# Compressed branch's readout with all 128 rows of the array: a block-sparse attention layer on one core

## The chip, the cores and the metric

The kernel runs on one core of one Trainium2 chip, as one launch. The time is device microseconds of an execution; the value of a kernel is the median of its runs. Of the engines, TensorE does the matmuls (each a weight load, "PEld" in the profile, and a pass of the moving operand, "PE"), VectorE (DVE), ScalarE (ACT) and GpSimd (POOL) do the rest, and SyncE (SP) issues most DMAs.

## What is computed

A trunk of two layers over 256 tokens of width 1024: a gated delta-rule layer (8 heads of 128), then an attention layer with 16 heads of 64 in 4 groups that share keys and values. The second layer has three branches, and its output is a gated sum of them. The change touches the compressed branch alone:

```python
p_cmp = masked_softmax(sc, cmp_end[None, :] <= t[:, None])
o_cmp = jnp.einsum('bgrqn,bgnd->bgrqd', p_cmp, v_cmp)
...
o = jnp.stack([o_cmp, o_sel, o_win], axis=2).astype(jnp.float32)
o = jnp.sum(gates[..., None] * o * jax.nn.silu(z.astype(jnp.float32)), axis=2).astype(x.dtype)
return o.reshape(b_sz, t_len, NSA_WIDTH) @ w_out
```

The keys and values of this branch are blocks of 32 tokens at a stride of 16, so there are 15 of them for 256 tokens; the kernel keeps 16 per head, the last one masked. With 4 blocks of 64 tokens and 16 to be chosen, the selection branch attends to all visible tokens.

## The kernel before

All activations are in float32. A projection is made of three matmuls on a high and a low part: L233 (high weights, high input), L234 (high weights, low input) and L235 (low weights, high input). Weights come as tiles of 128x1024 by DMA, ScalarE makes the high part (`hi_...`, L181) and GpSimd the low part (`lo_...`, L185). All engines but SyncE run in the order in which the program is written, so a list of small tasks is interleaved by hand: `fill(n)` takes the next n pieces of a projection from a list and puts them at this place of TensorE's order, and `defer(n, f)` puts a task n steps later.

In the attention of the second layer the work goes by units. A unit is a pair of heads for the first 128 tokens, or one head for the second 128. For each unit, in the order given by a string of digits: `scores` (L1327, TensorE), `maxima` (VectorE adds the mask and takes maxima, L1336 to L1343), `exps` (ScalarE, L1356 to L1361; `pt` holds the two long branches, `Pc` the compressed one), `transposes` (L1369 for the long branches, L1371 for `Pc`), `probs` (ScalarE copies the transposed probabilities out of PSUM, L1376 and L1380), and then, for each pair of heads, `readout`. Between them `fill` puts the pieces of the gate projection (`bz`) and of the output projection (`bo`).

`readout` multiplies the transposed probabilities by the values. The long branches take 4 or 8 matmuls with all 128 keys of a block as rows (L1395 for the first half of the tokens, L1398 for the second). The compressed branch takes one, L1401: the stationary operand is `PcT`, 32 rows (2 heads times 16 blocks) by 128 tokens, and the moving one is `vbd`, 32 rows by 130 columns, which holds the values of a group twice, block-diagonally over the two heads, with a column of ones in each for the denominator. The result of a readout goes into one PSUM bank (`op`), and `total` on VectorE (L1409 to L1413) divides, gates and adds the three branches. The next readout uses the same bank and waits for that.

`vbd` is a tile of 32 partitions; its columns of ones are written by GpSimd (L1106), its values by VectorE (L1195, in `compressed_v`). `PcT` is a rotating pair of tiles of 32 partitions, written by ScalarE (L1380). The 16 readouts lie between 249 and 377 us. Names that the text uses further: `th` (L1227) and `zz` (L1228) are the gate's activation, `lo_skv` is the low part of the weights of the shared keys and values, and L1157 is a matmul in the compression of the keys, whose operands have 125 rows.

Of the kernel before, what the change touches and what calls it, by code (L numbers as in the profile page):

```python
# [9 lines left out]
F32 = mybir.dt.float32  # L10
# [7 lines left out]
P = 128  # L18
# [75 lines left out]
def trunk(ctx: ExitStack, tc: tile.TileContext, I: dict, out: bass.AP):  # L94
    nc = tc.nc
    V, S, G, PE = nc.vector, nc.scalar, nc.gpsimd, nc.tensor
# [7 lines left out]
    def defer(n, f):  # L104
        late.append([n, f])
# [23 lines left out]
    wk = ph.enter_context(tc.tile_pool(name="wk", bufs=3))  # L129
# [116 lines left out]
    def fill(n, low=True):  # L246
        for _ in range(n):
            step()
            if fills:
                fills.pop(0)()  # L250
            if low:
                lower()
# [753 lines left out]
    def pool(name, bufs, **kw):  # L1006
        return ph.enter_context(tc.tile_pool(name=name, bufs=bufs, reuse_waits="tile", **kw))
# [5 lines left out]
    wk = pool("wkb", 2)  # L1013
# [8 lines left out]
    def tbank(name):  # L1022
        return pt_.tile([P, 512], F32, tag="t", name=name)
# [77 lines left out]
    G.memset(hpS, 0.0)  # L1101
    hid = wk.tile([P, 2, 4, 16], F32, name="hid", bufs=1)
    G.memset(hid, 0.0)
    vbd = wk.tile([32, 4, 2, 65], F32, name="vbd", bufs=1)
    bd = cb[0:32, C_BD:C_BD + 2]
    G.tensor_copy(vbd[:, :, :, 64], bd[:, None, :].to_broadcast([32, 4, 2]))  # L1106
    fill(2)
    k_post()
    fill(4)
# [76 lines left out]
    def compressed_v():  # L1186

        vcp = tbank("vcp")
        for g_ in range(4):
            PE.matmul(vcp[0:32, g_ * 64:(g_ + 1) * 64], hr[:, g_].rearrange("p a b -> p (a b)"), w2[:, 256:320],  # L1190
                      start=True, stop=True)

        def place():
            for g_ in range(4):
                V.tensor_tensor(vbd[:, g_, :, 0:64], vcp[0:32, None, g_ * 64:(g_ + 1) * 64].to_broadcast([32, 2, 64]),  # L1195
                                bd[:, :, None].to_broadcast([32, 2, 64]), op=ALU.mult)

        defer(1, place)
# [116 lines left out]
    S_, PT_, PTT, PC, PCT, MX, TP = {}, {}, {}, {}, {}, {}, {}  # L1315
# [57 lines left out]
    def probs(u):  # L1373
        t, h = u
        PT = PTT[u] = wk.tile([P, 2, 2, P], F32, tag="ra", name=f"PT{t}{h}", bufs=6)
        S.copy(PT.rearrange("p a b c -> p (a b c)"), TP[u])  # L1376
        if t == 0 or h % 2:
            h -= h % 2 * t
            PCT[t, h] = wk.tile([32, P], F32, tag="PcT", name=f"PcT{t}{h}", bufs=2)
            S.copy(PCT[t, h], S_[u][0:32, 1, 272:400])  # L1380

    OP, summed = {}, set()

# [102 lines left out]
    for i in range(n + 1):  # L1486
# [6 lines left out]
        if i:  # L1493
            probs(units[i - 1])
# [8 lines left out]
        if i:  # L1503
            t, h = units[i - 1]
# [95 lines left out]
```

## Time and profile before

| | |
|---|---|
| median of 3 runs | 393.53 us (392.84 to 394.13) |
| the profiled execution | 393.95 us |
| its span | 392.2 us |
| TensorE matmuls busy | 379.5 us, 97% |
| TensorE weight loads busy | 334.8 us, 85% |
| VectorE, ScalarE, GpSimd busy | 223.5, 220.4, 246.2 us |
| granted TensorE clock, mean | 0.995 |
| L1401 in the chain that ended last | 2% of the span |

A row of the timeline gives the start, the duration, the engine, the line, the operation, the tiles ("out<-in"), the rows and columns of the array that it uses ("32*128") and the moving operand's shape. In brackets stands the idle time before it and what ended that. A float32 matmul is two passes, each with a load of its own, so one call of L1401 shows as "x2". Matmuls are pipelined: the next one starts while the one before still counts as busy, so the pace is read from starts.

### The profile page before, as it was taken

To read this page: it belongs to the slowest core of one execution; us is meant where nothing else is said; L and a number is where in the kernel's file an instruction comes from. 1 tells how busy PE (TensorE), PEld (TensorE's weight loads), DVE (VectorE), ACT (ScalarE), POOL (GpSimd) and SP (SyncE) were. 2 spreads that over 40 slices of the span, in tenths; PEclk is the share of its full clock that TensorE was granted. 3 is DMA by queue.
4 is the path that set the end of the run, shared out by engine and by line. 5 is a ranking of instruction groups with operands and counts; after the bars stand their busy time and mean duration, and the time that the engine had idled before them with its cause. 6 is when DMAs were issued, how large, how long until landed. Compare 5 with 4: busy or idle time off the path is not lost.

```text
span 392.2 us, 7553 instructions
## 1 busy us (share of the span) xinstructions
PE 379.5 (97%) x2870; PEld 334.8 (85%) x2870; DVE 223.5 (57%) x591; ACT 220.4 (56%) x433; POOL 246.2 (63%) x154
## 2 busy tenths in 40 slices
PE   8999999999999999999999999999999999999991
PEld 6899999999979987877998788888888888878891
DVE  2868776678633455454541655645656465676726
ACT  4688766656654462625563649566474647456410
POOL 5699999747454846894754988193544637209051
PEclk9999999999999999999999999999999999999998
DMA  7876678754334315573636764343515243301011
GB/s 223 323 223 206 223 220 293 200 135 164 110 113 146 119 45 171 175 242 119 214 109 213 274 222 152 107 150 119 162 43 174 65 151 109 107 3 53 3 53 53
DMA packets 23476, 58.68 MB, mean 150 GB/s; under 512 B 6672, under 2 KB 9232, under 8 KB 23312
## 3 DMA queue, kind: packets, MB, share of 16 engines
q1 hardware_dynamic: 23232, 58.13, 44.7%
q8 instruction: 22, 0.36, 0.4%
q14 instruction: 14, 0.11, 0.1%
q10 hardware_dynamic: 144, 0.07, 0.1%
q0 software_dynamic: 64, 0.01, 0.0%
HBM read 55.96 MB, written 2.23 MB: 148 GB/s over the span
## 4 chain that ended last, share of the span: by engine, by line
PE 42%; DVE 4%; ACT 3%; DMA 2%; POOL 2%; issue 1%; POOLq 0%; DVEq 0%; SPq 0%; ACTq 0%
PE pbz L233 6%; PE pbz L234 6%; PE pbz L235 6%; PE op L1398 4%; PE s L1327 3%; PE ptp L1369 3%; DMA raw_bz<-in_bz 2%; PE op L1401 2%; PE op L1395 1%; ACT hi_bq L181 1%; POOL lo_bq L185 1%; PE pskv L235 1%; PE pbo L233 1%; PE pskv L233 1%; PE pskv L234 1%; PE qtp L1214 1%
## 5 line engine op out<-in xcount | busy, mean ns | idle before, releaser
L185 POOL TENSOR_TENSOR lo_bz<-raw_bz,hi_bz 128x1024 fp32r<-128x1024 f32 x24 | 56.8, 2390 | 39.1 <-ACT hi_bz L181 21.5
L185 POOL TENSOR_TENSOR lo_wqkv<-raw_wqkv,hi_wqkv 128x1024 fp32r<-128x1024 f32 x22 | 52.4, 2399 | 6.8 <-ACT hi_wqkv L181 4.7
L233 PE MATMUL pbz<-hi_bz,x1h 128*128 128x512 f32 x96 | 38.9, 405 | 0.0
L234 PE MATMUL pbz<-hi_bz,x1l 128*128 128x512 f32 x96 | 37.7, 393 | 0.0
L235 PE MATMUL pbz<-lo_bz,x1h 128*128 128x512 f32 x96 | 37.6, 392 | 0.0
L185 POOL TENSOR_TENSOR lo_bo<-raw_bo,hi_bo 128x1024 fp32r<-128x1024 f32 x8 | 18.8, 2384 | 22.8 <-ACT hi_bo L181 17.7
L185 POOL TENSOR_TENSOR lo_skv<-raw_skv,hi_skv 128x1024 fp32r<-128x1024 f32 x12 | 28.4, 2401 | 5.0 <-PE pskv L235 5.0
L185 POOL TENSOR_TENSOR lo_wz<-raw_wz,hi_wz 128x1024 fp32r<-128x1024 f32 x8 | 19.4, 2438 | 16.0 <-ACT hi_wz L181 15.9
L1376 ACT COPY PT<-ptp 128x512 f32<-128x512 f32 x24 | 14.1, 587 | 24.4 <-PE ptp L1369 24.4
L181 ACT CAST hi_bz<-raw_bz 128x1024 fp32r<-128x1024 f32 x24 | 25.3, 1053 | 2.9 <-DMA raw_bz<-in_bz 1.6
L185 POOL TENSOR_TENSOR lo_wo<-raw_wo,hi_wo 128x1024 fp32r<-128x1024 f32 x8 | 18.9, 2387 | 11.8 <-ACT hi_wo L181 11.8
L185 POOL TENSOR_TENSOR lo_bq<-raw_bq,hi_bq 128x1024 fp32r<-128x1024 f32 x8 | 19.1, 2394 | 11.6 <-ACT hi_bq L181 11.6
L181 ACT CAST hi_wqkv<-raw_wqkv 128x1024 fp32r<-128x1024 f32 x22 | 22.7, 1043 | 1.2 <-DMA raw_wqkv<-in_wqkv 1.2
L235 PEld LDWEIGHTS pbz<-lo_bz,x1h 128*128 128x128 f32 x96 | 18.0, 188 | 4.1
L233 PEld LDWEIGHTS pbz<-hi_bz,x1h 128*128 128x128 f32 x96 | 18.0, 188 | 4.1
L234 PEld LDWEIGHTS pbz<-hi_bz,x1l 128*128 128x128 f32 x96 | 18.0, 188 | 2.8
L1360 ACT ACTIVATE pt<-s,mx 128x256 f32<-128x256 f32 x32 | 13.4, 472 | 10.9 <-DVE mx L1343 8.7
L215 PE MATMUL pk<-xh,hi_wqkv 128*128 128x256 f32 x64 | 18.7, 292 | 0.0
L215 PE MATMUL pq<-xh,hi_wqkv 128*128 128x256 f32 x64 | 18.5, 289 | 0.0
L217 PE MATMUL pk<-xh,lo_wqkv 128*128 128x256 f32 x64 | 18.1, 283 | 0.0
L217 PE MATMUL pq<-xh,lo_wqkv 128*128 128x256 f32 x64 | 18.1, 283 | 0.0
L216 PE MATMUL pq<-xl,hi_wqkv 128*128 128x256 f32 x64 | 18.1, 283 | 0.0
(360 smaller groups left out, 1257.3 us busy)
## 6 DMA issues: line engine op xcount, KB each, us to landing
raw_bz<-in_bz SPq DMA_DIRECT2D x24, 512.0 KB, 3.3
raw_wqkv<-in_wqkv SPq DMA_DIRECT2D x23, 512.0 KB, 4.5
raw_skv<-in_skv SPq DMA_DIRECT2D x12, 512.0 KB, 3.3
raw_wz<-in_wz SPq DMA_DIRECT2D x8, 512.0 KB, 3.3
raw_wo<-in_wo SPq DMA_DIRECT2D x8, 512.0 KB, 3.4
raw_bq<-in_bq SPq DMA_DIRECT2D x8, 512.0 KB, 3.7
raw_bo<-in_bo SPq DMA_DIRECT2D x8, 512.0 KB, 3.3
raw_w<-in_w SPq DMA_DIRECT2D x4, 512.0 KB, 3.3
```

The lines of the kernel that those rows point to most:

```text
L181: S.copy(h, r)
L185: e.tensor_tensor(l, r, h.bitcast(F32), op=ALU.subtract)
L215: PE.matmul(ps[:, 0:T], wh[:, kt, :], ah[:, kt, :], start=kt == 0, stop=False)
L216: PE.matmul(ps[:, 0:T], wh[:, kt, :], al_[:, kt, :], start=False, stop=False)
L217: PE.matmul(ps[:, 0:T], wl[:, kt, :], ah[:, kt, :], start=False, stop=kt == 7)
L233: PE.matmul(ps, ah[:, kt, tt], wh[:, k4, cols], start=kt == 0, stop=False)
L234: PE.matmul(ps, al_[:, kt, tt], wh[:, k4, cols], start=False, stop=False)
L235: PE.matmul(ps, ah[:, kt, tt], wl[:, k4, cols], start=False, stop=kt == 7)
L1327: PE.matmul(sp[:, j, 0:n], lq, kk[:, hh // 4, c0:c0 + n], start=i == 0, stop=i == 1)
L1360: S.activation(pt[:, :, b, :], s4[:, :, b, :], AF.Exp, bias=mx[:, b:b + 1])
L1376: S.copy(PT.rearrange("p a b c -> p (a b c)"), TP[u])
L1398: PE.matmul(o3[:, r, 1 + b, :], PT[:, j, b, :], vt_[:, b, j, g_, :], start=j == 0, stop=j == 1)
```

## The change

`vbd` and the two tiles of `PcT` get all 128 partitions. GpSimd fills all three with zeros once, before the rest of the set-up; the writes go to the first 32 partitions as before. L1401, unchanged in the code, then reads 128 rows of both operands, of which 96 are zero. The two tiles of `PcT` are now made once and used in turn, instead of being taken from a rotating pair at each use. Five lines are added, so the lines behind them have numbers that are 5 higher in the changed kernel (L1401 is L1406 there).

```diff
-    vbd = wk.tile([32, 4, 2, 65], F32, name="vbd", bufs=1)
+    vbd = wk.tile([P, 4, 2, 65], F32, name="vbd", bufs=1)
+    G.memset(vbd, 0.0)
+    pct = [wk.tile([P, P], F32, name=f"PcT{i}", bufs=1) for i in range(2)]
+    for c_ in pct:
+        G.memset(c_, 0.0)
     bd = cb[0:32, C_BD:C_BD + 2]
-    G.tensor_copy(vbd[:, :, :, 64], bd[:, None, :].to_broadcast([32, 4, 2]))
+    G.tensor_copy(vbd[0:32, :, :, 64], bd[:, None, :].to_broadcast([32, 4, 2]))
...
             for g_ in range(4):
-                V.tensor_tensor(vbd[:, g_, :, 0:64], vcp[0:32, None, g_ * 64:(g_ + 1) * 64].to_broadcast([32, 2, 64]),
+                V.tensor_tensor(vbd[0:32, g_, :, 0:64], vcp[0:32, None, g_ * 64:(g_ + 1) * 64].to_broadcast([32, 2, 64]),
                                 bd[:, :, None].to_broadcast([32, 2, 64]), op=ALU.mult)
...
-            PCT[t, h] = wk.tile([32, P], F32, tag="PcT", name=f"PcT{t}{h}", bufs=2)
-            S.copy(PCT[t, h], S_[u][0:32, 1, 272:400])
+            PCT[t, h] = pct[len(PCT) % 2]
+            S.copy(PCT[t, h][0:32, :], S_[u][0:32, 1, 272:400])
```

On GpSimd, in the set-up of the attention layer, before the change (`hid` is a fill of the compression, `vbd<-cb` the columns of ones, `lo_skv` the weights that follow; in brackets what an instruction waits for):

```order
L1103 MEMSET hid 128x128
L1106 COPY vbd<-cb 32x8 [waits DMAHW5_49]
L185 TENSOR_TENSOR lo_skv_2432<-raw_skv_2290,hi_skv_2431 128x1024 [waits DMAHW4_49,PE_49,Activation_49]
L185 TENSOR_TENSOR lo_skv_2444<-raw_skv_2302,hi_skv_2443 128x1024 [waits DMAHW7_49,PE_49,Activation_49]
L185 TENSOR_TENSOR lo_skv_2456<-raw_skv_2314,hi_skv_2455 128x1024 [waits DMAHW0_49,PE_49,Activation_49]
```

and with the change:

```order
L1103 MEMSET hid 128x128
L1106 MEMSET vbd 128x520
L1109 MEMSET PcT_2388 128x128
L1109 MEMSET PcT_2389 128x128
L1111 COPY vbd<-cb 32x8 [waits DMAHW5_49,Pool_49]
L185 TENSOR_TENSOR lo_skv_2437<-raw_skv_2290,hi_skv_2436 128x1024 [waits DMAHW4_49,PE_49,Activation_49]
L185 TENSOR_TENSOR lo_skv_2449<-raw_skv_2302,hi_skv_2448 128x1024 [waits DMAHW7_49,PE_49,Activation_49]
```

Three fills stand ahead of the copy and of the four `lo_skv`; nothing else on GpSimd moved. VectorE's order is the same; its write of the values into `vbd` (L1195) now waits for GpSimd as well.

On TensorE, at a readout of the first half of the tokens among the gate projection's pieces (`vtok` are the values of the long branches, `PT` their transposed probabilities), before:

```order
L1395 MATMUL op_3153<-vtok,PT_3135 128x65 [waits Activation_49]
L1395 MATMUL op_3153<-vtok,PT_3135 128x65 x3
L1401 MATMUL op_3153<-vbd,PcT_3137 128x2x65 [waits Activation_49]
L233 MATMUL pbz_3099<-hi_bz_3085,x1h 128x512
L234 MATMUL pbz_3099<-hi_bz_3085,x1l 128x512
```

and with the change:

```order
L1400 MATMUL op_3157<-vtok,PT_3140 128x65 [waits Activation_49]
L1400 MATMUL op_3157<-vtok,PT_3140 128x65 x3
L1406 MATMUL op_3157<-vbd,PcT_2388 128x2x65 [waits Activation_49]
L233 MATMUL pbz_3104<-hi_bz_3090,x1h 128x512
L234 MATMUL pbz_3104<-hi_bz_3090,x1l 128x512
```

The same instructions stand in the same order with the same waits; no instruction is added or taken away on TensorE, and what differs, the rows of the operands, is not in these rows.

## Rows read from the trace of the kernel before

**Rows 1.** Page, part 1: busy us (share of the span) and instructions, by engine.

```profile
PE 379.5 (97%) x2870; PEld 334.8 (85%) x2870; DVE 223.5 (57%) x591; ACT 220.4 (56%) x433; POOL 246.2 (63%) x154
```

**Rows 2.** Stretches: engines' busy us (instructions), granted TensorE clock, DMA share, GB/s.

```profile
247.00:336.00 89.00, 89.00 (x511) 76.11 (x510) 49.15 (x115) 52.44 (x120) 47.26 (x20) 1.00 0.36 119
336.00:350.00 14.00, 13.12 (x86) 10.81 (x85) 11.89 (x31) 7.18 (x20) 0.00 (x0) 1.00 0.11 40
350.00:376.00 26.00, 26.00 (x175) 23.22 (x174) 15.00 (x38) 14.38 (x32) 12.61 (x8) 1.00 0.06 21
380.00:392.00 12.00, 4.36 (x37) 4.15 (x35) 6.60 (x14) 0.37 (x1) 1.70 (x2) 0.85 0.15 54
```

**Rows 3.** Stretches, TensorE's instructions of line L1401 alone.

```profile
247.00:328.00 81.00, 4.85 (x20) 2.92 (x20) 1.00 0.33 111
350.00:380.00 30.00, 1.46 (x6) 0.88 (x6) 1.00 0.08 31
```

**Rows 4.** Timeline at the first readout: start us, us, engine, line, operation, tiles, count.

```profile
249.01 0.39 PE L1395 MATMUL op<-vtok,PT 128*128 128x65 f32 x2
...
249.12 0.28 PE L1395 MATMUL op<-vtok,PT 128*128 128x65 f32 x1
249.32 0.29 PEld L1401 LDWEIGHTS op<-vbd,PcT 32*128 32x128 f32 x2
...
249.43 0.18 PEld L1401 LDWEIGHTS op<-vbd,PcT 32*128 32x128 f32 x1
...
249.74 0.19 PEld L233 LDWEIGHTS pbz<-hi_bz,x1h 128*128 128x128 f32 x1
250.08 0.39 PE L234 MATMUL pbz<-hi_bz,x1l 128*128 128x512 f32 x1
250.30 0.39 PE L235 MATMUL pbz<-lo_bz,x1h 128*128 128x512 f32 x1
```

**Rows 5.** Timeline at line L1157, 125 rows of the array between projections.

```profile
216.15 0.39 PE L235 MATMUL pbq<-lo_bq,x1h 128*128 128x512 f32 x1
216.16 0.42 PEld L1157 LDWEIGHTS hp<-cb,hpS 125*128 125x128 f32 x2
...
216.39 0.19 PEld L1157 LDWEIGHTS hp<-cb,hpS 125*128 125x128 f32 x1
...
216.50 0.19 PEld L233 LDWEIGHTS pbq<-hi_bq,x1h 128*128 128x128 f32 x1
```

**Rows 6.** Timeline at a readout with transposes behind it.

```profile
333.79 0.28 PE L1398 MATMUL op<-vtok,PT 128*128 128x65 f32 x1
...
334.80 0.19 PEld L1327 LDWEIGHTS s<-kh,qT 128*128 128x128 f32 x1
```

**Rows 7.** Chain that ended last, 340.5 to 350 us: start us, us, what.

```profile
341.00 0.61 ACT th L1227
...
344.51 2.00 PE op L1398 x16
...
346.51 0.43 PE op L1401 x2
...
349.21 0.88 PE op L1398 x6
```

**Rows 8.** Timeline at the readout of 365 us.

```profile
364.99 0.84 ACT L1360 ACTIVATE pt<-s,mx 128x256 f32<-128x256 f32 x2
...
365.87 0.14 PEld L1369 LDWEIGHTS ptp<-ident,pt 128*128 128x128 f32 x1
```

**Rows 9.** GpSimd: a fill in the list of groups, and the timeline at 183 us.

```profile
L696 POOL MEMSET XT<- 128x1024 f32 x2 | 1.9, 950 | 0.0
...
183.17 2.41 POOL L185 TENSOR_TENSOR lo_skv<-raw_skv,hi_skv 128x1024 fp32r<-128x1024 f32 x1 [4.98 <-PE pskv L235]
```

**Rows 10.** Timeline: the last split of a projection's weights, and its first user.

```profile
317.98 2.39 POOL L185 TENSOR_TENSOR lo_bz<-raw_bz,hi_bz 128x1024 fp32r<-128x1024 f32 x1 [3.32 <-ACT hi_bz L181]
...
320.60 0.19 PEld L235 LDWEIGHTS pbz<-lo_bz,x1h 128*128 128x128 f32 x1
```

## Prediction, made before the changed kernel ran

> **What bounds the kernel now.** I read the page's busy table first: TensorE's matmuls are busy for 97% of the span [rows 1]. A pipelined matmul counts as busy until its modelled end, so this says that TensorE never stands idle for long, not that it works at its peak. The table by stretches comes next. The changed matmul runs from 249 us on, and from 247 to 336 us and from 350 to 376 us the busy time fills the stretch completely, at a granted clock of 1.00; only between 336 and 350 us is TensorE short of it, 13.12 of 14 us [rows 2]. So whatever TensorE saves before 336 us or after 350 us comes off the end, as long as the other engines still deliver in time; between the two it must be looked at piece by piece.
>
> Then the line itself. L1401 runs once in each of 16 readouts, as two passes with a weight load each; 20 of the 32 passes come before 328 us, 6 after 350 us [rows 3]. The timeline of the first readout shows what one costs [rows 4]. Its load is written "32*128", 32 rows of the array and all 128 columns, and takes 0.18 us where the loads of 128 rows beside it take 0.19; durations show nothing wrong, so look at the starts. There is the steady state first: two passes of L1395 start at 249.01 and 249.12, 0.11 apart, and two of the projection (L234, L235) at 250.08 and 250.30, about 0.23 apart. Between 249.12 and 250.08 lie only three more starts, the two passes of L1401 and L233. At the steady pace L234 would start 3 x 0.11 + 0.23 = 0.56 us after 249.12. It starts 0.96 us after. **0.40 us are lost around a 0.4 us instruction**, in two halves. The first load of L1401 begins at 249.32, 0.20 after the last pass of L1395 began. The second load of L1401 begins at 249.43 and the next one, L233's, only at 249.74, which is 0.31 later where 0.11 is the pace: 0.20 more. Every fast stretch has its loads running ahead under the matmul before; at the two borders of L1401 the load waits until the matmul before has drained.
>
> Is it the 32 rows? The same trace has a matmul that answers this, L1157, with 125 rows and 120 columns, between two projections [rows 5]. Its first load begins at 216.16, 0.01 after the start of the pass before, and L233's load begins at 216.50, 0.11 after its second load at 216.39. No border, no loss. A matmul that occupies nearly all rows is entered and left at the steady pace.
>
> **The change, part by part.** TensorE's order stays as it is; only the operands of L1401 grow to 128 rows (the added ones hold zeros).
>
> *Readouts followed by a projection.* 12 of 16. Saved: 0.40 as read off above to the hundredth; I take 0.39. Ten of them are the 20 passes up to 328 us, in the full stretch: 10 x 0.39 = 3.90. Two more lie behind 350 us: 0.78. The unknown is the price of an L1401 of 128 rows. Its lower bound is the pace of L1395, 0.11 per pass [rows 4], because the load of 128 columns sets it there. Its upper bound is that nothing is saved, should the loss belong to something other than the rows. I take the lower bound, as L1157 is nearest in kind and in columns.
>
> *Readouts followed by transposes.* Four, at 334, 342, 346 and 365 us. At 334 us [rows 6] the last pass of L1398 starts at 333.79 and the load of the scores L1327 at 334.80, 1.01 later. Two passes of L1401 and four transposes, each paced by a load of 128 columns as L1395 is, take 6 x 0.11 = 0.66, so 0.35 is saved.
> At 342 us nothing is: the chain of work runs from the activation L1227 (341.00) through VectorE to L1398 at 344.51, and L1401 is not on it [rows 7]. At 346 us the chain does pass through L1401 (346.51) and goes on to VectorE and to L1398 at 349.21 [rows 7]; only the border in front of L1401 counts there: 0.20. At 365 us the transposes begin at 365.87, while the exponential that they need ended at 364.99 + 0.84 = 365.83 [rows 8]; they cannot come earlier. The front border, 0.20, still reaches VectorE sooner, and that sets the next unit. I take 0.20 between the ends 0 and 0.35.
>
> The Trainium skill has a rule against all this. In "TensorE: Matmul & The Clock Gate", section "LDWEIGHTS (loading the stationary operand)", a weight load costs by its columns alone, the same for 32 rows as for 128, and the section on what overlaps lets loads run under a matmul only where the row groups differ. By it padding gains nothing and the sum is 0. The trace agrees on the load's duration and not on the overlap: 128-row loads run under 128-row matmuls throughout rows 4.
>
> *Three zero fills on GpSimd*, ahead of lo_skv. A fill of 128x1024 takes 0.95 us [rows 9]; the three together have 776 columns, so they take between 0.72 us (by columns) and 2.85 us (the whole of that row for each). GpSimd stands idle for 4.98 us right behind them, waiting for TensorE, until 183.17 [rows 9]. Cost 0. Without that cover the first lo_skv, and TensorE behind it, would be later by as much. VectorE's writes into vbd now also wait for these fills; they belong to a stage behind all of lo_skv.
>
> *ScalarE's copy of PcT* writes the same 32 rows as before and alternates over two buffers as before: 0.
>
> **The sum.** 3.90 + 0.35 + 0 + 0.20 + 0.78 + 0.20 = 5.43 us. The profiled execution took 393.95 us, 1.75 us outside its span of 392.2 included; it becomes 388.5. It stands 0.4 us over the median of the runs, 393.53, from which I count: **388.1 us**, about 1.4% faster. Its own range is 387.3 (all 16 readouts in full: 12 x 0.39 + 4 x 0.35 = 6.1) to 389.0 (0.07 less in each of ten readouts and 0.2 less behind them).
>
> **The rivals.**
> *One border only.* If the load of L1401 runs ahead, but the one behind it still waits, or the other way round, each readout saves 0.20 and the one at 342 us nothing: 15 x 0.20 = 3.0, 390.5 us. Against it: L1157 loses at neither end. Chance 0.07.
> *The lead is taken by what comes late next.* TensorE gets ahead of the weights. At the last projection of this stage lo_bz ends at 317.98 + 2.39 = 320.37, and its first user loads at 320.60, 0.23 later [rows 10]; one more readout saves more than that. If the weights and exponentials set the pace from there on, the readouts behind 308 us (four, about 1.5 us) give nothing: 389.6 us. Against it: these chains start from TensorE's own scores, so they move forward with it. Chance 0.08.
> *It does nothing*, because the wait belongs to the semaphore on PcT, to vbd or to the output's layout, or by the page's rule above: 393.5 us. For it: the load's duration does not depend on rows. Against it: L1157, and the border behind L1401, where the next instruction, L233, is of another kind. Chance 0.05.
> *Slower, by the clock.* Between 336 and 350 us TensorE already waits, 0.88 of 14 us [rows 2], and the change lengthens these waits, by 0.35 at 342 us and 0.20 at 346 us, to 1.4 us. In the tail, with 4.36 busy of 12 us, the granted clock is down to 0.85 on average [rows 2]. Should it fall to 1.2 GHz at 342 us, each following us of bound TensorE work would cost up to another: above about 5.4 us at the low level the gain is gone, and with 10 us there the time is 393.5 + 4.6 = 398.1. Against it: the clock stands at 1.00 over this stretch with waits of the same kind. Chance 0.02.
>
> **How the numbers follow.** Forecast 0.78, then 0.07, 0.08, 0.05 and 0.02. The range 386.9 to 390.0 holds the forecast with the spread of the three runs (0.6 either way) at its low end, and the late-weights case; it leaves out the one-border case, no change and slower, 0.14. About 0.3%, 1.2 us, can be told from no change here. Faster by more than that: 0.78 + 0.07 + 0.08 = 0.93. Within: 0.05. Slower: 0.02.
>
> **What would show it.** In the changed profile L1401's loads (line 1406 there) read "128*128" and start 0.05 after the pass in front; L234 starts 0.56 us after the last pass of L1395, not 0.96; from 336 to 350 us TensorE's wait for L1413 grows; lo_skv still starts after an idle time, of about 4 us. The prediction is wrong if the loads still start 0.20 late, or if they do not and the end moves by less than 4 us: then the list of TensorE's waits must name the new one.

## The result, and the profile after

The changed kernel takes 388.96 us (median of 6 runs, 388.02 to 389.60), the kernel before, run beside it, 393.91 us (6 runs, 392.84 to 394.88). The ratio is 0.9875, with a 95% interval of 0.9855 to 0.9895: 4.9 us less (4.1 to 5.7), where 5.4 us were forecast. The profiled execution took 389.49 us.

Of the page, the span and the busy times of TensorE; they answer to [rows 1]:

```profile
span 387.7 us, 7558 instructions
...
PE 374.2 (97%) x2870; PEld 332.2 (86%) x2870; DVE 223.2 (58%) x591; ACT 220.5 (57%) x433; POOL 247.0 (64%) x157
```

The span is 4.5 us shorter and TensorE is as full as before, 97%, with the same 2870 passes. The same stretches as in [rows 2] (engines' busy us and instructions, then the granted clock):

```profile
247.00:336.00 89.00, 89.00 (x529) 77.30 (x528) 52.12 (x122) 54.41 (x128) 47.34 (x20) 1.00 0.37 125
336.00:350.00 14.00, 13.08 (x87) 10.96 (x86) 10.77 (x28) 8.25 (x20) 1.15 (x1) 1.00 0.01 2
350.00:376.00 26.00, 26.00 (x188) 24.03 (x187) 15.15 (x39) 11.59 (x27) 14.20 (x10) 1.00 0.11 39
```

The clock stands at 1.00 in all three. From 336 to 350 us TensorE is busy for 13.08 us, where it was 13.12: the hole has moved forward with the rest and has hardly grown.

The first readout, which answers to [rows 4] (start us, us, engine, line, operation, tiles, rows and columns of the array, count):

```profile
248.98 0.28 PE L1400 MATMUL op<-vtok,PT 128*128 128x65 f32 x1
...
249.03 0.30 PEld L1406 LDWEIGHTS op<-vbd,PcT 128*128 128x128 f32 x2
249.09 0.44 PE L1406 MATMUL op<-vbd,PcT 128*128 128x130 f32 x2
...
249.26 0.19 PEld L233 LDWEIGHTS pbz<-hi_bz,x1h 128*128 128x128 f32 x1
...
249.37 0.19 PEld L234 LDWEIGHTS pbz<-hi_bz,x1l 128*128 128x128 f32 x1
...
249.60 0.40 PE L234 MATMUL pbz<-hi_bz,x1l 128*128 128x512 f32 x1
```

L1406 now reads "128*128". Its first load begins at 249.03, 0.05 after the last pass of L1400 began, and L233's at 249.26, 0.23 after it for two steps; before the change that way was 0.42. No load waits here any longer. L234 passes at 249.60, 0.62 after the last L1400; it was 0.96. So 0.34 us are saved, and not the 0.40 that the prediction read off.

The readout with transposes behind it, once at 334 us [rows 6]:

```profile
330.50 0.30 PEld L1406 LDWEIGHTS op<-vbd,PcT 128*128 128x128 f32 x2
...
330.73 0.47 PEld L1374 LDWEIGHTS ptp<-ident,pt 128*128 128x128 f32 x4
...
331.16 0.19 PEld L1332 LDWEIGHTS s<-kh,qT 128*128 128x128 f32 x1
```

From L1406's first load to the load of the scores it is now 0.66 us, and the transposes' loads run on from 330.73 without a gap. At 334 us in the kernel before, the first load of L1401 came 0.20 after the pass in front of it, at 333.99, and the scores' load at 334.80.

GpSimd behind the fills; the last row answers to [rows 9]:

```profile
178.13 0.53 POOL L1106 MEMSET vbd<- 128x520 f32 x1
178.61 0.35 POOL L1109 MEMSET PcT<- 128x128 f32 x2
...
183.26 2.39 POOL L185 TENSOR_TENSOR lo_skv<-raw_skv,hi_skv 128x1024 fp32r<-128x1024 f32 x1 [4.17 <-PE pskv L235]
```

The fills take 0.53 us and twice about 0.2 us, and 4.17 us of the idle time are left before lo_skv, which again starts when TensorE lets it.

### The profile page after: what moved, and what is told of

Same layout as the page of the kernel before. It is cut to its first block, busy times and chain, and to the rows that moved or that the text cites. A ratio compares the mean times of both kernels' runs of the same rounds, so it can differ in the third digit from the quotient of the medians.

```text
span 387.7 us, 7558 instructions
## 1 busy us (share of the span) xinstructions
PE 374.2 (97%) x2870; PEld 332.2 (86%) x2870; DVE 223.2 (58%) x591; ACT 220.5 (57%) x433; POOL 247.0 (64%) x157
## 4 chain that ended last, share of the span: by engine, by line
PE 87%; DMA 3%; DVE 3%; POOL 3%; issue 1%; ACT 1%; SPq 1%; POOLq 0%; DVEq 0%; ACTq 0%
PE pbz L235 6%; PE pbz L233 6%; PE pbz L234 6%; PE op L1403 4%; PE s L1332 3%; PE ptp L1374 3%; PE pwz L233 2%; PE pk L217 2%; PE pk L215 2%; PE pwo L235 2%; PE pq L215 2%; PE pq L216 2%; PE pq L217 2%; PE pk L216 2%; PE pwo L233 2%; PE pwo L234 2%
## 5 line engine op out<-in xcount | busy, mean ns | idle before, releaser
L233 PE MATMUL pbz<-hi_bz,x1h 128*128 128x512 f32 x96 | 38.7, 403 | 0.0
L235 PE MATMUL pbz<-lo_bz,x1h 128*128 128x512 f32 x96 | 37.8, 394 | 0.0
L234 PE MATMUL pbz<-hi_bz,x1l 128*128 128x512 f32 x96 | 37.6, 392 | 0.0
L235 PEld LDWEIGHTS pbz<-lo_bz,x1h 128*128 128x128 f32 x96 | 18.0, 188 | 4.3 <-POOL lo_bz L185 0.2
L234 PEld LDWEIGHTS pbz<-hi_bz,x1l 128*128 128x128 f32 x96 | 18.1, 188 | 2.8
L233 PEld LDWEIGHTS pbz<-hi_bz,x1h 128*128 128x128 f32 x96 | 18.1, 188 | 2.8
L217 PE MATMUL pk<-xh,lo_wqkv 128*128 128x256 f32 x64 | 18.2, 285 | 0.0
L217 PE MATMUL pq<-xh,lo_wqkv 128*128 128x256 f32 x64 | 18.1, 283 | 0.0
```

The costliest lines, as they stand in the source:

```text
L217: PE.matmul(ps[:, 0:T], wl[:, kt, :], ah[:, kt, :], start=False, stop=kt == 7)
L233: PE.matmul(ps, ah[:, kt, tt], wh[:, k4, cols], start=kt == 0, stop=False)
L234: PE.matmul(ps, al_[:, kt, tt], wh[:, k4, cols], start=False, stop=False)
L235: PE.matmul(ps, ah[:, kt, tt], wl[:, k4, cols], start=False, stop=kt == 7)
```

## The experiments

**How many rows.** Three kernels differ from the changed one only in how much of the padded tiles L1406 reads; the fills, the tiles and the fixed pair stay. The diff of the first:

```diff
-        PE.matmul(o3[:, :, 0, :], PCT[t, h], vbd[:, g_, :, :], start=True, stop=True)
+        PE.matmul(o3[:, :, 0, :], PCT[t, h][0:32, :], vbd[0:32, g_, :, :], start=True, stop=True)
```

and with 64 and 96 in place of 32 in the other two.

32 rows. Expected:

> The changed kernel with all its fills, larger tiles and fixed PcT pair, but L1406 reads only the first 32 rows of both operands, as before the change. If the gain belongs to the 32 rows of the array, all of it is gone: 393.9 us (392.8 to 394.6), and the first load of the line starts 0.20 us after the pass before, the load behind it 0.31 after its second. If the gain came from anything else in the change (the tiles' places, the fixed pair, the waits), the time stays at 389.0 us.

Measured: 393.10 us against 393.02 before, ratio 1.0004 (0.9993 to 1.0014). All of the gain is gone, and the borders are back. At the first readout the last load of L1400 starts at 247.91, and then:

```profile
248.17 0.29 PEld L1406 LDWEIGHTS op<-vbd,PcT 32*128 32x128 f32 x2
...
248.58 0.19 PEld L233 LDWEIGHTS pbz<-hi_bz,x1h 128*128 128x128 f32 x1
...
248.92 0.39 PE L234 MATMUL pbz<-hi_bz,x1l 128*128 128x512 f32 x1
```

In front it is 0.26 us from load to load, and from the first load of L1406 to L233's 0.41 for two steps, where 0.11 is the pace of one.

64 rows. Expected:

> The same with 64 rows. If every border between a part of the array's rows and all of them costs the drain, the loss stays whole or nearly: 392.5 to 394 us. If the loss goes with the number of empty rows, about two thirds of it: 392.2 us. If 64 rows count as full, 389.0 us. The 64-row matmuls that the kernel has elsewhere speak for the first: the load behind them starts 0.147 us after their last pass where others start at once.

Measured: 393.26 us, ratio 1.0004 (0.9994 to 1.0014). The same place:

```profile
248.03 0.29 PEld L1406 LDWEIGHTS op<-vbd,PcT 64*128 64x128 f32 x2
...
248.44 0.19 PEld L233 LDWEIGHTS pbz<-hi_bz,x1h 128*128 128x128 f32 x1
...
248.78 0.39 PE L234 MATMUL pbz<-hi_bz,x1l 128*128 128x512 f32 x1
```

From the first load to L234 it is 0.75 us with 32 rows and 0.75 us with 64. Nothing of the loss goes with the number of empty rows.

96 rows. Expected:

> The same with 96 rows. By borders between row groupings (32 and 64 are such groupings, 96 is none) nothing is lost: 389.0 us, and the first load starts 0.05 us after the pass before. If the loss goes with the number of empty rows, a third of it stays: 390.6 us. If only the full 128 rows escape, 392.5 to 394 us.

Measured: 388.92 us, ratio 0.9888 (0.9874 to 0.9903). The same place:

```profile
249.50 0.30 PEld L1406 LDWEIGHTS op<-vbd,PcT 96*128 96x128 f32 x2
...
249.73 0.19 PEld L233 LDWEIGHTS pbz<-hi_bz,x1h 128*128 128x128 f32 x1
...
250.08 0.39 PE L234 MATMUL pbz<-hi_bz,x1l 128*128 128x512 f32 x1
```

0.58 us, as with 128 rows (0.57, from 249.03 to 249.60). So it is not a question of full or empty, but of 32 and 64 rows on one side and 96, 125 [rows 5] and 128 on the other. This settles the cause: everything else of the change is in the first two kernels too, and they are as slow as the kernel before. The rival by which the wait belonged to PcT's semaphore, to vbd or to the layout of the output falls with them, since all three are the same in these kernels.

The Trainium skill states this drain: "TensorEngine Tiling (Array Packing)", section "Key Properties", says that a change of the tiling mode, and not of the tile alone, drains TensorE; its section "Available Configurations" lists groupings of 32 and 64 rows beside the whole. The traces agree: the load in front waits until 0.20 us after the start of the pass before it, and the one behind comes 0.20 us late; that 96 rows count as the whole is shown here by the run with 96, and the Trainium skill does not say it. The rule of the Trainium skill that the prediction weighed, from "TensorE: Matmul & The Clock Gate", section "The mechanism" (loads run under a matmul only where row groups differ), does not hold in this trace as it stands: 128-row loads run under 128-row passes, in the changed kernel L1406's at 249.03 under the pass of 248.98, and in the kernel before L1401's second load, at 249.43 [rows 4], starts 0.11 after its first, under a pass of the same 32 rows. What waits is the first load behind a change from all rows to 32 or back.

**The excursion twice.** One head's part of the matmul is issued ahead of the long branches' matmuls, the other's behind them, so that each readout has the 32-row excursion twice; the same cut was run with 32 rows and with 128:

```diff
+        def part(r):
+            PE.matmul(o3[:, r, 0, :], PCT[t, h][0:32, :], vbd[0:32, g_, r, :], start=True, stop=True)
+
+        if half != 0:
+            part(0)
         for r in range(2) if half is None else (half,):
...
-        PE.matmul(o3[:, :, 0, :], PCT[t, h], vbd[:, g_, :, :], start=True, stop=True)
+        part(1)
```

Expected with 32 rows:

> 32 rows, and the matmul cut in two of 65 columns: one head's part ahead of the long branches' matmuls, the other's behind them, so each readout leaves the full array twice. The cut itself costs two more passes, 2 x 0.11 less the 0.05 that 130 columns take longer than a load: 0.17 us. With a drain at each border, 0.17 + 0.34 = 0.51 us more for each readout that TensorE bounds, 12 to 15 of them: 6.1 to 7.7 us, 399 to 401 us. If the drain is paid once per readout only, or belongs to the 130 columns, 395 to 396 us.

Expected with 128 rows:

> The same cut with 128 rows: only the two passes more, 0.17 us in 12 to 15 readouts, so 2.0 to 2.6 us over the changed kernel: 391.0 to 391.6 us. With e7 this gives the price of two excursions: by the theory of the borders e7 minus e8 is 8 to 9 us, twice what the change saved; otherwise 4 us as between the two kernels as they are.

Measured: 401.92 us with 32 rows, ratio 1.0221 (1.0196 to 1.0246), and 392.73 us with 128, ratio 0.9985 (0.9972 to 0.9998). Their difference is 9.2 us, against 4.9 between the two kernels with one excursion: about twice. Both lie about 1 us above the ranges expected for them. The first readout with 32 rows:

```profile
248.52 0.39 PE L235 MATMUL pbz<-lo_bz,x1h 128*128 128x512 f32 x1
248.83 0.29 PEld L1397 LDWEIGHTS op<-vbd,PcT 32*128 32x128 f32 x2 [0.36 <-issue]
...
249.19 0.97 PEld L1405 LDWEIGHTS op<-vtok,PT 128*128 128x128 f32 x8
...
250.23 0.29 PEld L1397 LDWEIGHTS op<-vbd,PcT 32*128 32x128 f32 x2
...
250.59 0.19 PEld L233 LDWEIGHTS pbz<-hi_bz,x1h 128*128 128x128 f32 x1
...
250.93 0.40 PE L234 MATMUL pbz<-hi_bz,x1l 128*128 128x512 f32 x1
```

and with 128 (same columns):

```profile
247.79 0.40 PE L235 MATMUL pbz<-lo_bz,x1h 128*128 128x512 f32 x1
247.79 0.42 PEld L1397 LDWEIGHTS op<-vbd,PcT 128*128 128x128 f32 x2
...
248.13 0.97 PEld L1405 LDWEIGHTS op<-vtok,PT 128*128 128x128 f32 x8
...
249.60 0.39 PE L234 MATMUL pbz<-hi_bz,x1l 128*128 128x512 f32 x1
```

From L235 in front to L234 behind it is 2.41 us with 32 rows and 1.81 us with 128: 0.60 for two excursions. In the first fence each of the four borders shows: L1397's first load comes 0.31 after L235's start. L1405's, at 249.19, comes 0.36 after that one, which is 0.25 after L1397's second load, where 0.11 is the pace. Behind the eight long loads L1397 waits again, until 250.23, and L233's load at 250.59 comes once more 0.36 after it. The estimate for the cut itself was low: two more passes cost 0.11 each in full, so 1.81 against 1.57 with one uncut matmul (the same measure, in the changed kernel). It is so in eleven of the 16 readouts, 0.21 to 0.23 us each by the loads. The other part of the excess is a new wait: at the ninth readout the part that now goes ahead waits 0.48 us for `PcT`, until 311.97, and that readout grows by 0.77; the ones at 342 and 365 us do not grow. So it is 392.7 us and not 391.0 to 391.6.

**Which readouts pay.** A counter gives 128 rows to some readouts and 32 to the others:

```diff
-        PE.matmul(o3[:, :, 0, :], PCT[t, h], vbd[:, g_, :, :], start=True, stop=True)
+        cnt["ro"] = cnt.get("ro", 0) + 1
+        k = 128 if cnt["ro"] <= 10 else 32
+        PE.matmul(o3[:, :, 0, :], PCT[t, h][0:k, :], vbd[0:k, g_, :, :], start=True, stop=True)
```

Expected for the first ten:

> 128 rows in the first ten readouts only (249 to 327 us), 32 rows in the last six. If every readout in the full stretch gives the 0.336 us that its starts show, 10 x 0.336 = 3.4 us under the kernel before: 389.6 us where that has 393.0. By the prediction's 0.39 it would be 389.1 us. If the lead were taken by late weights from 308 us on, about 1 us less: 390.6 us.

Measured: 389.93 us against 393.25 before, ratio 0.9924 (0.9901 to 0.9947): 3.3 us less, with 3.4 expected. The late-weights rival, 390.6 us, lies within the interval, which reaches to 391.2, so the time alone does not exclude it. The trace does: readout after readout adds its 0.32 to 0.35 us to the lead, the last of the ten included, and between the ninth and the tenth only 0.06 of it is lost again.

With `cnt["ro"] in (11, 12, 13, 15)`, the four with transposes behind them, expected:

> 128 rows only in the four readouts with transposes behind them (334, 342, 346 and 365 us), 32 rows in the other twelve. By the prediction's reading of the chain: 0.35 + 0 + 0.20 + 0.20 = 0.75 us under the kernel before; by the starts in the changed kernel's trace 0.3 + 0 + 0.15 + 0.1 = 0.55 us: 392.4 us where before has 393.0. If all four counted in full, 4 x 0.35 = 1.4 us: 391.6 us.

Measured: 392.98 us, ratio 0.9988 (0.9971 to 1.0004): between 1.1 us less and 0.2 us more. 1.4 us for the four in full lies outside; 0.55 and 0.75 cannot be told apart by the time. The trace of this run says more: the line's first load in the tenth readout is at 326.45 in the kernel before and at 325.43 here, 1.02 earlier, as in the eight readouts in front of it, which have 32 rows in both; in the sixteenth it is at 376.28 and 374.68, 1.60 earlier. So the four give 0.58 together, near the 0.55 of the starts.

**The cover of the fills.** `G.memset(vbd, 0.0)` stands 17 times in a row:

```diff
-    G.memset(vbd, 0.0)
+    for _ in range(17):
+        G.memset(vbd, 0.0)
```

Expected:

> The changed kernel with vbd filled 17 times, not once: 16 more fills of about 0.48 us, some 7.7 us of GpSimd work in place of an idle time of 4.4 us, so the first lo_skv starts about 3.4 us later, near 186.6 us. As the prediction had it, TensorE is then later by as much: 392.3 us. Rival: the idle time is not the only cover, since in the trace the first user of lo_skv loads 5.2 us after that tile is done; then nothing moves: 389.0 us (within 0.6).

Measured: 388.97 us, ratio 0.9890 (0.9874 to 0.9906), no later than the changed kernel. Of the timeline, the first lo_skv and its first user:

```profile
188.63 2.38 POOL L185 TENSOR_TENSOR lo_skv<-raw_skv,hi_skv 128x1024 fp32r<-128x1024 f32 x1
...
191.07 0.19 PEld L217 LDWEIGHTS pc<-x1h,lo_skv 128*128 128x128 f32 x1
```

lo_skv starts 5.4 us later than in the changed kernel (3.4 were expected; the 17 fills take 9.97 us, 0.59 each and not 0.48) and ends at 191.01; its user loads at 191.07. The idle time was the smaller half of the cover: behind it the finished tile lay 5.2 us before it was used, from 185.65 to the load of L217 at 190.88 in the changed kernel.

**The other lone 32-row matmul.** L368 near 14 us gets 96 rows with zeros, on top of the change:

```diff
+    G.memset(pair, 0.0)
     add_pairs(16)
+    ba = wk.tile([96, T], F32, tag="sq", name="ba", bufs=2)
+    G.memset(ba, 0.0)
...
-    ba = wk.tile([32, T], F32, tag="sq", name="ba", bufs=2)
-    V.tensor_copy(ba, gps[0:32, T:2 * T])
+    V.tensor_copy(ba[0:32, :], gps[0:32, T:2 * T])
...
-                PE.matmul(gps[:, t * 16:(t + 1) * 16], ba[:, t * P:(t + 1) * P], pair[0:32, 0:16], start=True, stop=True)
+                PE.matmul(gps[:, t * 16:(t + 1) * 16], ba[:, t * P:(t + 1) * P], pair[0:96, 0:16], start=True, stop=True)
```

Expected:

> The changed kernel, and the same padding at the only other lone 32-row matmul between 128-row ones, L368 near 14 us: its operands get 96 rows, with zeros behind the 32. By the theory of the borders, the second L365 pass behind it starts some 0.63 us after the last one in front of it, not 0.98, and 0.3 to 0.35 us come off the end: 388.6 us where the changed kernel has 389.0, too little for the interval to show. If the theory holds only at L1406, the starts stay.

and for the changed kernel beside it:

> The changed kernel again, beside the one before and the padded one on one chip: 0.9875 of the kernel before, as at first.

Measured: 388.73 us padded, ratio 0.9883 (0.9863 to 0.9903), and 389.01 us as changed, ratio 0.9886 (0.9866 to 0.9905), both against 393.30. The padded one (the line is L370 there):

```profile
13.82 0.28 PE L367 MATMUL pv<-xl,hi_wqkv 128*128 128x256 f32 x1
13.83 0.53 PEld L370 LDWEIGHTS gps<-pair,ba 96*128 96x128 f32 x4
...
14.31 0.36 PE L367 MATMUL pv<-xh,hi_wqkv 128*128 128x256 f32 x1
...
14.51 0.28 PE L367 MATMUL pv<-xl,hi_wqkv 128*128 128x256 f32 x1
```

and the changed kernel that ran beside it, in the same stretch:

```profile
14.20 0.28 PE L365 MATMUL pv<-xl,hi_wqkv 128*128 128x256 f32 x1
14.41 0.52 PEld L368 LDWEIGHTS gps<-pair,ba 32*128 32x128 f32 x4
...
14.96 0.39 PE L365 MATMUL pv<-xh,hi_wqkv 128*128 128x256 f32 x1
...
15.18 0.28 PE L365 MATMUL pv<-xl,hi_wqkv 128*128 128x256 f32 x1
```

The second L365 (L367) behind the group starts 0.69 us after the last one in front of it, and 0.98 us in the changed kernel: 0.29 us less, just under the 0.3 to 0.35 expected. The times cannot show it: the padded kernel is no slower, what it saves at this place is read from the starts alone, and whether that reaches the end is not shown.

## Why the prediction was right, and where its size was off

*The mechanism* held at every point that was tried: the loss sits at the two borders of L1401, it belongs to the rows (32 and 64 have it, 96 and 128 do not), and the time fell by what TensorE stopped losing, since TensorE is the bound nearly everywhere behind 249 us.

*The step that was off* is the term "Readouts followed by a projection. ... I take 0.39". Each gave 0.34. The ten up to 328 us were put at 3.90 and measure 3.3, in the trace and in the run with the first ten alone; the two behind 350 us were put at 0.78 and measure 0.67. The mistake was in reading the pace. "At the steady pace L234 would start 3 x 0.11 + 0.23 = 0.56 us after 249.12" adds the starts of two kinds of passes. In the changed kernel's first readout above, a short pass (L1406, at 249.09) starts 0.06 after its own load, while that load still runs; the 512-column pass L234 starts 0.23 after its load (249.37, 249.60), when the stream in front of it is through. From a start of the first kind to one of the second the way is 0.06 longer. Loads compared with loads would have given the right number. The first readout of the kernel before again, with the two loads that stand around those of [rows 4]:

```profile
249.06 0.19 PEld L1395 LDWEIGHTS op<-vtok,PT 128*128 128x128 f32 x1
...
249.85 0.19 PEld L234 LDWEIGHTS pbz<-hi_bz,x1l 128*128 128x128 f32 x1
```

From L1395's last load at 249.06 to L1401's first at 249.32 it is 0.26, which is 0.15 over the pace of 0.11; from L1401's second load at 249.43 to L233's at 249.74 it is 0.31, 0.20 over; L234's follows at the pace. Together that is 0.79 for four steps, where the same four take 0.45 in the changed kernel: 0.34 too much. The border at the back had been read rightly; the one in front was measured from a pass, which itself begins 0.06 after its load. (The load of 249.06, under the pass of 249.01, is also the row for "128-row loads run under 128-row matmuls", which the prediction placed in [rows 4]; those rows have none.)

*Readouts followed by transposes.* 0.35 was taken at 334 us. From the projection's pass in front of the readout to the second transpose it measures 2.63 us before and 2.34 us after, 0.29. The same reading was off by the same 0.06.

At 342 us "nothing is" saved: confirmed, by the chain that the prediction named and by a second wait that it did not. From L235 in front to the second transpose it is 1.81 us before and 1.82 us after. ScalarE's exponential and the transposes' loads there:

```profile
338.24 0.48 ACT L1365 ACTIVATE pt<-s,mx 128x256 f32<-128x256 f32 x1
...
338.40 0.14 PEld L1374 LDWEIGHTS ptp<-ident,pt 128*128 128x128 f32 x1
...
338.76 0.31 PEld L1374 LDWEIGHTS ptp<-ident,pt 128*128 128x128 f32 x3 [0.23 <-ACT pt L1365]
```

The second load waits for the exponential, whose last part ends at 338.24 + 0.48 = 338.72, and starts at 338.76. On TensorE the saved time has become this wait.

At 346 us the chain of waits still runs over L1398 (L1403 now), L1401 (L1406) and VectorE; its first row is L1227 (now L1232) of the named chain:

```profile
337.39 0.61 ACT th L1232
...
340.87 2.00 PE op L1403 x16
...
342.87 0.29 PE op L1406 x2
...
345.44 1.11 PE op L1403 x8
```

From the activation to L1403 it is 3.48 us, as it was 3.51 from 341.00 to 344.51 [rows 7]: nothing saved there. From 340.87 to 345.44 it is 4.57 us; it was 4.70, from 344.51 to 349.21 [rows 7]. 0.13 and not 0.20: the border in front costs 0.15 there too, not 0.20, within the hundredths of the rows.

At 365 us "they cannot come earlier" was right:

```profile
360.88 0.84 ACT L1365 ACTIVATE pt<-s,mx 128x256 f32<-128x256 f32 x2
...
361.56 0.53 PEld L1374 LDWEIGHTS ptp<-ident,pt 128*128 128x128 f32 x4
```

The exponential ends at 360.88 + 0.84 = 361.72, and of the transposes only the first load comes early, at 361.56. The two traces lie 0.1 us further apart behind this place than in front of it, where 0.20 were taken. The prediction's sign that TensorE's wait for L1413 would grow did not come true: two waits, 0.6 us, in both kernels.

*The sum.* 3.3 + 0.3 + 0 + 0.1 + 0.7 + 0.1 = 4.5, with rounded terms, against 4.5 us between the spans and 4.9 between the medians. None of the sixteen came out above its forecast, and nearly all of the shortfall is the border in front, read as 0.20 and measured as 0.15. It is read from the starts; the medians alone do not show it, since 5.4 us lies within their interval. That they came within 0.5 us of the forecast is in part scatter (the last paragraph of this section). The low end of the sum's own range, 387.3, is 387.45 by its terms, 393.53 - 6.08; nothing hangs on it.

*The rivals.* One border only: no, the loads run on at both. Late weights: the ten readouts keep their lead, but the place that the rival named does show. The load of L235 that came 0.23 us behind lo_bz before [rows 10] now waits for it:

```profile
317.70 0.19 PEld L235 LDWEIGHTS pbz<-lo_bz,x1h 128*128 128x128 f32 x1 [0.25 <-POOL lo_bz L185]
```

The lead, 3.08 us in front of this place, is 3.02 behind it: 0.06 lost, and the readouts that follow add to it as before.

It does nothing: no. The clock: 1.00 in the stretch in question, and TensorE's idle time there is 0.92 us, where it was 0.88. The zero fills cost 0, as forecast; but "without that cover the first lo_skv, and TensorE behind it, would be later by as much" was wrong in its second half, as the run with 17 fills shows.

The difference of the medians (4.9) is larger than that of the spans (4.5). Both lie within the interval, and in the later run of the same two kernels the medians lie 4.3 us apart (393.30 and 389.01), so the scatter of the medians alone covers it.

## What to carry to other kernels

A float32 matmul that used 32 or 64 rows of the array, alone among matmuls of 128, cost about 0.34 us beyond its own passes here, because the loads at both its ends waited; zeros in the other rows, written once, took that away, and 96 rows were enough. Its own duration looks innocent in a list of groups: look at the starts of the loads around it, and compare loads with loads, since passes start at different distances from their loads. Then ask, for each place, whether TensorE is what the next work waits for: twelve of sixteen places gave 4.0 of the 4.5 us here, and one gave nothing because an exponential was due at the same moment.

## What was not expected of the hardware

64 rows cost as much as 32 (0.75 us from the first load to L234, in both), and 96 as little as 128 (0.58 and 0.57 us). The expectations of these runs had it so; the prediction had only 32 and 125 rows to go by. The kernel before has a 96-row matmul of its own, L1297, between matmuls of 128 rows, and it shows no border either:

```profile
240.77 0.53 PEld L1297 LDWEIGHTS gq<-pair,gf 96*128 96x128 f32 x4
241.22 0.19 PEld L1327 LDWEIGHTS s<-kh,qT 128*128 128x128 f32 x1
```

From its first load to the load behind its four it is 0.45 us, four steps at the pace.

Nor is it rows alone. In the kernel before, L1142 uses 128 rows and 61 columns: its first load, at 208.15, comes 0.31 us after the start of the pass in front (207.84), for no wait that the profile shows, and L233's load behind it starts at 210.05 after an idle time of 0.17. These look like the same borders. The transposes L1371, with 128 rows and 32 columns, have no border: their load at 252.90 is followed by that of L1327 at 253.01. L1142 is in two passes a matmul and L1371 in one; whether that makes the difference no run here tests.

An added pass of 65 columns on the whole array costs 0.11 us, which is the pace of the loads, not of the columns: two of them made a readout longer by 0.24 us.
